# Shared PSUM banks in the mixer of a two-block model, and 30 convolution taps handed to the attention loop

## The chip, the cores and the metric

The kernel runs on one core of a Trainium2 chip. What counts is the device time of one execution in microseconds (us). Three executions of the kernel before took 4014.26, 4025.6 and 4031.81 us, the median is 4025.6 us. In the profile PE is TensorE's matmuls, PEld its weight loads, DVE is VectorE, ACT ScalarE, POOL GpSimd and SP the engine that issues most DMAs.

## The reference

Two blocks run one after the other on 512 tokens of width 1024. The change touches the second one only, in both of its layers. A layer there is a mixer followed by an MLP, and the mixer has three branches that read the same normalized input:

```python
h = rms_norm_2(x, pre_mix_w[l])
u = h @ w_in[l]
(u_conv, dq, dk, dv, gqkv, gz, b_f, b_b, a_f, a_b) = jnp.split(u, offs, axis=-1)
y_conv  = conv_module(u_conv, ...)      # 256 channels, gate, depthwise conv of 31 taps, layer norm, silu
y_diff  = diff_attention(dq, dk, dv, ...)  # 6 heads, two softmaxes each, o = (p0 - lam*p1) @ v
y_delta = gated_deltanet(gqkv, gz, ...)    # 6 heads, both directions, chunks of 64
y = jnp.concatenate([y_conv, y_diff, y_delta], axis=-1) @ w_out[l]
x = x + rms_norm_2(y, post_mix_w[l])
```

In the delta branch each chunk of 64 tokens needs a triangular solve (`u`, `w`), and a scan carries a state over the 8 chunks:

```python
v_new = u_i - w_i @ state
o     = qg_i @ state + aqk_i @ v_new
state = state * gl_i + kdec_i.T @ v_new
```

## The kernel before

**Stages of the mixer.** `second(l)` writes one mixer as a program in this order, where the numbers 0, 1, 2 are pairs of delta heads: the gates and the projections of pair 0; `delta_prep(0)`, its rest and the projections of pair 1; `delta_prep(1)` and its rest; `conv_proj`; `delta_uw(0)`; the projections of pair 2; `conv_taps`; `delta_prep(2)`; `delta_scan(0)`; `delta_uw(1)`; two `dense_tok` (z and v, 384 columns each); `diff_proj` (q and k of the attention); `delta_out(0)`, `delta_scan(1)`, rest of 2, `delta_uw(2)`, `delta_out(1)`, `delta_scan(2)`, `delta_out(2)`; last `diff`, the differential attention in 24 blocks (6 heads times 4 query blocks), with `conv_norm` inside it after the second pair of heads. After that the output projection reads all branches from DRAM (`cat`).

**What sets the order.** The program is written in that order, but a scheduler (the tile context is opened with `schedule_with_timeline_sim=True`) then gives each engine its own fixed list of instructions. It prefers what is earlier in the program, and takes later work where the earlier is not ready or its tile has no free slot. A tile pool has slots by tag; the tiles of one tag share them. Each engine runs its list strictly in order.

**PSUM.** There are 8 banks of 128x512 words. In the mixer before they are four pools of two: `mm` (projections, the attention's values `po`), `fx` (two of the four `dense_tok` outputs, transposes after the short convolution, the attention's scores and its transposes), `ax` (nearly all of the delta branch) and `sA` (the running state of the scan). So the delta branch and the attention never ask for the same bank.

**The delta branch** is a chain. In `delta_uw` each of two directions runs: 32 small matmuls (L1559), a DVE copy `AT`, 64 matmuls (L1569, L1570), the DVE update `TZ` (L1571), then twice 8 matmuls (L1583), a DVE `Q`, 8 matmuls (L1592), a DVE `Z` (L1593), and 16 matmuls (L1604) that ACT evacuates. `delta_scan` has 416 matmuls of 64x64 as the trace counts them and 7 steps that go PE, copy on DVE or ACT (L1650, L1652), PE. `delta_out` squares on ACT (L1694), makes a reciprocal root in some 13 short DVE instructions, multiplies, and transposes (L1707).

**The convolution** keeps two halves of 128 channels. Half z=0 is accumulated by one DVE instruction a tap (L1743, 30 of them after a first one on ACT), half z=1 by ACT (L1746, into the one buffer `cm`) and POOL (L1747).

**The attention.** A block is: two score matmuls into `fx` (L1840), per score one DVE instruction that adds the bias and takes the extreme (L1842) and one ACT exponential (L1844), the combination of the two softmaxes (on DVE L1862, in every third block ACT L1859 and POOL L1860), four transposes into `fx` (L1866), an ACT copy `dat`, and four matmuls with the values (L509). The loop runs one block ahead:

```python
scores(0)
for b in range(nb):
    if b + 1 < nb:
        scores(b + 1)
    outputs(b)
```

Of the kernel before, what the change touches and what calls it, by code (L numbers as in the profile page):

```python
# [9 lines left out]
F32 = mybir.dt.float32  # L10
# [3 lines left out]
AF = mybir.ActivationFunctionType  # L14
ALU = mybir.AluOpType
AX = mybir.AxisListType
PSUM = bass.MemoryType.PSUM
P = 128
# [103 lines left out]
class Rows:  # L122


    def __init__(self, a, b, c0=0, c1=768):
        self.t, self.c0, self.c1 = (a, b), c0, c1
# [32 lines left out]
class Slots:  # L159
# [6 lines left out]
    def tile(self, shape, dt, tag, name, bufs=1):  # L166
        n = int(np.prod(shape[1:]))
        if n < P:
            return self.pool.tile(shape, dt, tag=tag, name=name, bufs=bufs)
        t = self.slots[self.n % len(self.slots)][:, :n]  # L170
        self.n += 1
        names = "abcd"[:len(shape) - 1]
        return t.rearrange(f"p ({' '.join(names)}) -> p {' '.join(names)}", **dict(zip(names, shape[1:])))


class Kern:
# [12 lines left out]
    def tap(self, name, ap):  # L189
        if self._tap is not None and name in self._tap:  # L190
            self.nc.sync.dma_start(self._tap[name], ap)
# [1536 lines left out]
    def conv_taps(self, l, pool, hd):  # L1728
        nc = self.nc
        hp = pool.tile([P, 2, 544], F32, tag="hp", name="hp")  # L1730
        nc.gpsimd.memset(hp[:, :, 0:15], 0.0)
        nc.gpsimd.memset(hp[:, :, 527:544], 0.0)
        nc.sync.dma_start(hp[:, :, 15:527], hd)
        acc = pool.tile([P, 2, 512], F32, tag="cacc", name="cacc")
        for z in range(2):
            w = lambda t: self.dw[:, l, t, z:z + 1]
            a = acc[:, z]
            bias = self.vec("conv_dw_b_2", 2 * l + z, 1)
            nc.scalar.activation(a, hp[:, z, 0:512], AF.Identity, bias=bias, scale=w(0))
            for t in range(1, 31):  # L1740
                v = hp[:, z, t:t + 512]
                if z == 0:
                    nc.vector.scalar_tensor_tensor(out=a, in0=v, scalar=w(t), in1=a, op0=ALU.mult, op1=ALU.add)  # L1743
                else:
                    m = pool.tile([P, 512], F32, tag="cm", name="cm", bufs=1)
                    nc.scalar.activation(m, v, AF.Copy, scale=w(t))  # L1746
                    nc.gpsimd.tensor_tensor(out=a, in0=a, in1=m, op=ALU.add)  # L1747
        self.load["act"] += 31 * 480
        self.load["dve"] += 31 * 600
        self.load["pool"] += 31 * 1200  # L1750
        return acc

    def conv_norm(self, l, pool, acc, cat):
        nc = self.nc
# [37 lines left out]
                        nc.sync.dma_start(qk[f][z, g], x)  # L1792
                self.dense_fm(self.I["w_in_2"][l], [(c0 + P * f, P)], [hsrc], ev)

    def diff(self, l, pool, qk, vd, cat, between):

        nc = self.nc
# [27 lines left out]
        def scores(b):  # L1827
            hd, qb = b // 4, b % 4
            if qb == 0:
                head(hd)  # L1830
            s = heads[hd]
            if b % 2 == 0:
                blocks[b // 2] = (self.p_raw.tile([P, 2048], F32, tag="raw", name="dP").rearrange("p (q m c) -> p q m c", q=2, m=2),
                                  self.p_whl.tile([P, 1024], F32R, tag="wl", name="dat").bitcast(F32).rearrange("p (q k c) -> p q k c", q=2, k=4))
            pe = blocks[b // 2][0][:, b % 2]
            o0 = 384 - P * qb
            for m in range(2):
                ps = self.psf()
                t = s["qk"][m]
                nc.tensor.matmul(ps, t[:, qb * P:(qb + 1) * P], t[:, 512:], start=True, stop=True)  # L1840
                mx = s["mx"][:, qb, m:m + 1]
                nc.vector.tensor_tensor_reduce(out=pe[:, m], in0=ps, in1=s["bias"][:, o0:o0 + 512], scale=1.0, scalar=3.0e38,  # L1842
                                               op0=ALU.add, op1=ALU.min, accum_out=mx)
                nc.scalar.activation(pe[:, m], pe[:, m], AF.Exp, bias=mx, scale=-1.0, accum_out=s["sm"][:, qb, m:m + 1])  # L1844
            self.load["dve"] += 1300
            self.load["act"] += 1050
# [33 lines left out]

        nb = 24
        scores(0)
        for b in range(nb):
            if b + 1 < nb:
                scores(b + 1)
            outputs(b)

    def second_consts(self, pool, tmp):
        nc, I = self.nc, self.I
# [84 lines left out]
    def second(self, l):  # L1974
        tc, nc, I = self.tc, self.nc, self.I
        pd = self.p_dram
        w = I["w_in_2"][l]
# [4 lines left out]
        qk = [pd.tile([2, 4, P, 512], F32, tag=f"qk{l}{f}", name="qk") for f in range(3)]  # L1982
        cat = pd.tile([P, KT, 512], F32, tag=f"cat{l}", name="cat")
        p_ps = ExitStack()
        self.pd, self.pf, self.px, psa = (p_ps.enter_context(tc.tile_pool(name=f"{t}{l}", bufs=2, space=PSUM))
                                          for t in ("mm", "fx", "ax", "sA"))
        p_cv, cv, p_hs = self.p_cv, self.cv, self.p_hs
        nc.sync.dma_start(xs, self.x)
        self.p_x.close()
# [36 lines left out]
        self.conv_proj(l, pool, hs, hd)  # L2026
        uw(0)
        tok[2] = self.delta_proj(l, 2, pool, hs)
        acc = self.conv_taps(l, cv, hd)
        self.level(*BAL[1])  # L2030
        prep(2)
        scan(0)
# [13 lines left out]
        self.level(0, 0, 100)  # L2046
        out(2)
        self.level(*BAL[2])
        self.diff(l, rb, qk, vd, cat, lambda f: self.conv_norm(l, rb, acc, cat) if f == 1 else None)
        p_rb.close()  # L2050
        p_cv.close()
        p_dl.close()
# [309 lines left out]
```

## Time and profile before

| | |
|---|---|
| three runs, median | 4025.6 us (4014.26 to 4031.81) |
| profiled execution | 4036.42 us, its span 4034.6 us |
| PE, DVE, ACT, POOL busy | 3704.7, 2440.8, 1571.0, 1669.0 us |
| first mixer, gates to the last attention output | 2267 to 2673 us |
| second mixer, the same | 3167 to 3571 us |

The rows quoted further down are of one execution. A row "x30: 735/752/2862, 2331.5 to 2395.9" means 30 instructions, their shortest, median and longest duration in ns, and the start of the first and of the last in us from the span's start. PE's busy time is modelled from pipelined matmuls; a stretch with a granted clock (PEclk) of 1.00 runs at 2.4 GHz, one with 0.50 at 1.2 GHz.

### The profile page before, as it was taken

Reading aid. Unit: us, or ns where it says so; the run is one execution under the profiler, and the core shown is the slowest. Engines: PE = TensorE matmul, PEld = TensorE weight load, DVE = VectorE, ACT = ScalarE, POOL = GpSimd, SP = SyncE. Lnnn points to the kernel's source line nnn. Section 1 sums busy time; section 2 is a strip of 40 time slices with the busy share of each in tenths; the row PEclk is TensorE's granted clock in tenths of the full one; section 3 lists DMA queues with packets and bytes.
Section 4 is the critical chain, followed back from the end, with each engine's and each line's share of the span. In section 5 each row is a group of like instructions: output and inputs, shape, how many; then the busy total and the mean of one; then the engine's idle time right before and its main releaser. Section 6 shows DMA issues by size and latency. Waiting matters only on the chain. (4 is left out here: it accounts for less than half of the span.)

```text
span 4034.6 us, 67160 instructions
## 1 busy us (share of the span) xinstructions
PE 3704.7 (92%) x27441; PEld 3287.6 (81%) x27441; DVE 2440.8 (60%) x4507; ACT 1571.0 (39%) x2654; POOL 1669.0 (41%) x1168
## 2 busy tenths in 40 slices
PE   8999989989998999997999988878999988878998
PEld 6888767989998788887999876768988776778988
DVE  6454566665666333336776684548767685558665
ACT  4544255323223222223343543444434443344433
POOL 2221225455553223233666454215554363115654
PEclk8999879989999999998999987879999887878999
DMA  6322444112222212121232433132334333132333
GB/s 208 93 77 78 155 130 157 43 53 65 72 73 77 66 58 71 60 84 51 84 115 88 118 99 119 52 113 94 105 105 122 92 101 104 55 123 92 105 97 112
DMA packets 420364, 379.79 MB, mean 94 GB/s; under 512 B 64586, under 2 KB 366169, under 8 KB 419161
## 3 DMA queue, kind: packets, MB, share of 16 engines
q1 hardware_dynamic: 414490, 367.01, 29.4%
q10 hardware_dynamic: 5567, 8.49, 0.6%
q8 instruction: 216, 3.54, 0.4%
q14 instruction: 91, 0.75, 0.1%
HBM read 332.21 MB, written 43.25 MB: 93 GB/s over the span
## 5 line engine op out<-in xcount | busy, mean ns | idle before, releaser
L206 ACT CAST wh<-raw 128x1024 fp32r<-128x1024 f32 (+2 forms) x441 | 444.6, 1014 | 630.9 <-PE mm L486 277.6
L233 POOL TENSOR_TENSOR wl<-raw,wh 128x1024 fp32r<-128x1024 f32 (+2 forms) x196 | 468.1, 2397 | 530.7 <-ACT wh L206 476.5
L233 DVE TENSOR_TENSOR wl<-raw,wh 128x1024 fp32r<-128x1024 f32 (+1 forms) x268 | 378.1, 1415 | 189.1 <-ACT wh L206 176.4
L485 PE MATMUL mm<-Hh,wh 128*128 128x512 f32 (+1 forms) x1256 | 417.5, 335 | 15.3 <-DVE x L1033 12.9
L487 PE MATMUL mm<-Hh,wl 128*128 128x512 f32 (+1 forms) x1256 | 417.0, 333 | 0.5 <-DVE wl L233 0.5
L486 PE MATMUL mm<-Hl,wh 128*128 128x512 f32 (+1 forms) x1256 | 416.3, 332 | 0.0
L485 PEld LDWEIGHTS mm<-Hh,wh 128*128 128x128 f32 x1256 | 238.7, 190 | 42.9 <-DVE x L1033 14.3
L487 PEld LDWEIGHTS mm<-Hh,wl 128*128 128x128 f32 x1256 | 238.8, 190 | 26.1 <-DVE wl L233 0.7
L486 PEld LDWEIGHTS mm<-Hl,wh 128*128 128x128 f32 x1256 | 239.0, 190 | 24.3
L485 PE MATMUL mm<-hh,wh 128*128 128x512 f32 (+1 forms) x640 | 231.9, 366 | 16.4 <-DVE hh L208 6.9
L509 PE MATMUL mm<-hl,wh 128*128 128x256 f32 (+1 forms) x808 | 231.5, 290 | 6.4 <-DVE hl L1960 6.3
L509 PE MATMUL mm<-hh,wl 128*128 128x256 f32 (+1 forms) x808 | 231.6, 290 | 5.5 <-DVE wl L233 4.1
L487 PE MATMUL mm<-hh,wl 128*128 128x512 f32 (+1 forms) x640 | 227.2, 357 | 2.8 <-POOL wl L233 2.8
L486 PE MATMUL mm<-hl,wh 128*128 128x512 f32 (+1 forms) x640 | 229.0, 359 | 0.6 <-DVE hl L698 0.6
L509 PE MATMUL mm<-hh,wh 128*128 128x256 f32 (+1 forms) x808 | 218.4, 288 | 6.5 <-ACT hh L1968 3.2
L206 ACT CAST wh<-s 128x1024 fp32r<-128x1024 f32 (+1 forms) x128 | 106.9, 835 | 267.4 <-PE mm L486 137.6
L509 PE MATMUL mm<-th,wh 128*128 128x256 f32 (+1 forms) x644 | 195.3, 305 | 8.1 <-ACT wh L206 5.5
L509 PE MATMUL mm<-th,wl 128*128 128x256 f32 (+1 forms) x644 | 197.3, 307 | 3.1 <-DVE wl L233 3.1
L1033 DVE SCALAR_TENSOR_TENSOR x<-mm,mod,x 128x512 f32<-128x512 f32 (+1 forms) x224 | 138.2, 630 | 99.9 <-PE mm L487 99.4
L509 PE MATMUL mm<-tl,wh 128*128 128x256 f32 (+1 forms) x644 | 195.3, 303 | 0.6 <-DVE tl L233 0.6
L233 POOL TENSOR_TENSOR Hl<-o,Hh 128x1024 fp32r<-128x1024 f32 (+3 forms) x76 | 140.9, 1856 | 92.6 <-ACT Hh L206 91.1
L509 PEld LDWEIGHTS mm<-hl,wh 128*128 128x128 f32 (+1 forms) x808 | 155.8, 193 | 9.7 <-DVE hl L1960 7.7
(737 smaller groups left out, 10886.8 us busy)
## 6 DMA issues: line engine op xcount, KB each, us to landing
raw<-in_w_ff_dram SPq DMA_DIRECT2D x68, 1024.0 KB
raw<-in_ffn_w_in_dram SPq DMA_DIRECT2D x88, 512.0 KB
raw<-in_mod_w_dram SPq DMA_DIRECT2D x40, 1024.0 KB
raw<-in_odd_w_in_dram SPq DMA_DIRECT2D x24, 1024.0 KB
raw<-in_ffn_w_out_dram SPq DMA_DIRECT2D x19, 1024.0 KB
raw<-in_w_in_dram SPq DMA_DIRECT2D x38, 512.0 KB
dqk<-qk SPq DMA_DIRECT2D x48, 256.0 KB
raw<-in_w_out_dram SPq DMA_DIRECT2D x12, 768.0 KB
```

The lines of the kernel that those rows point to most:

```text
L206: nc.scalar.copy(hi, src)
L233: i = (nc.vector if e == "dve" else nc.gpsimd).tensor_tensor(out=out, in0=a, in1=b, op=op)
L485: mm(ps, ah, bh, start=first, stop=False)
L486: mm(ps, ah, bl, start=False, stop=False)
L487: mm(ps, al, bh, start=False, stop=last)
L509: i = self.nc.tensor.matmul(out, lhsT, rhs, start=start, stop=stop, skip_group_check=True)
L1033: self.nc.vector.scalar_tensor_tensor(out=x[:, ct, :n], in0=ps, scalar=gate[:, ct:ct + 1], in1=x[:, ct, :n], op0=ALU.mult, op1=ALU.add)
```

## The change

The pools `fx`, `ax` and `sA` become one pool with the single tag `any` and six banks; `mm` keeps its two. Whatever tag a caller names, its tile comes from those six. The scores run two blocks ahead in place of one. `conv_taps` starts both halves on ACT, issues the whole half z=1 as before, and returns the 30 DVE taps of z=0 as functions; `diff` calls two of them after each of its first 15 blocks. Names and arithmetic stay; in the changed file lines are 10 later up to `conv_taps`, the tap on DVE is L1756, the score matmul L1846, the transposes of the attention L1872.

```diff
+class OneTag:
+    def __init__(self, pool):
+        self.pool = pool
+
+    def tile(self, shape, dt, tag, name):
+        return self.pool.tile(shape, dt, tag="any", name=name)
...
+        w = lambda t, z: self.dw[:, l, t, z:z + 1]
         for z in range(2):
-            w = lambda t: self.dw[:, l, t, z:z + 1]
-            a = acc[:, z]
-            bias = self.vec("conv_dw_b_2", 2 * l + z, 1)
-            nc.scalar.activation(a, hp[:, z, 0:512], AF.Identity, bias=bias, scale=w(0))
-            for t in range(1, 31):
-                v = hp[:, z, t:t + 512]
-                if z == 0:
-                    nc.vector.scalar_tensor_tensor(out=a, in0=v, scalar=w(t), in1=a, op0=ALU.mult, op1=ALU.add)
-                else:
-                    m = pool.tile([P, 512], F32, tag="cm", name="cm", bufs=1)
-                    nc.scalar.activation(m, v, AF.Copy, scale=w(t))
-                    nc.gpsimd.tensor_tensor(out=a, in0=a, in1=m, op=ALU.add)
...
+            nc.scalar.activation(acc[:, z], hp[:, z, 0:512], AF.Identity, bias=self.vec("conv_dw_b_2", 2 * l + z, 1), scale=w(0, z))
+        for t in range(1, 31):
+            m = pool.tile([P, 512], F32, tag="cm", name="cm", bufs=1)
+            nc.scalar.activation(m, hp[:, 1, t:t + 512], AF.Copy, scale=w(t, 1))
+            nc.gpsimd.tensor_tensor(out=acc[:, 1], in0=acc[:, 1], in1=m, op=ALU.add)
...
+        def tap(t):
+            nc.vector.scalar_tensor_tensor(out=acc[:, 0], in0=hp[:, 0, t:t + 512], scalar=w(t, 0), in1=acc[:, 0], op0=ALU.mult, op1=ALU.add)
+        return acc, [lambda t=t: tap(t) for t in range(1, 31)]
...
         scores(0)
+        scores(1)
         for b in range(nb):
-            if b + 1 < nb:
-                scores(b + 1)
+            if b + 2 < nb:
+                scores(b + 2)
             outputs(b)
+            for f in fill[2 * b:2 * b + 2]:
+                f()
...
-        self.pd, self.pf, self.px, psa = (p_ps.enter_context(tc.tile_pool(name=f"{t}{l}", bufs=2, space=PSUM))
-                                          for t in ("mm", "fx", "ax", "sA"))
+        self.pd, ps = (p_ps.enter_context(tc.tile_pool(name=f"{t}{l}", bufs=n, space=PSUM)) for t, n in (("mm", 2), ("any", 6)))
+        self.pf = self.px = psa = OneTag(ps)
```

The instruction lists of the engines show where the scheduler puts all this. The first place is PE at the end of the first mixer's delta branch. Before, scores (L1840, `fx<-dqk`), attention transposes (L1866) and values (`mm<-dv,dat`) stand among the last pair's `delta_prep` (L1446, L1463, L1475) and the first scan (`sA`, L1637):

```order
L509 MATMUL sA<-U,kd 64x64 x14
L1840 MATMUL fx<-dqk 128x512 x2
L1446 MATMUL ax<-gd,dm 128x512
L1463 MATMUL ax<-eb,dm 128x512
L1475 MATMUL ax<-kT 64x64 x8
L1866 MATMUL fx<-ident,dP 128x128 x4
L1840 MATMUL fx<-dqk 128x512
L509 MATMUL mm<-dv,dat 128x64 x4
L1840 MATMUL fx<-dqk 128x512
L1866 MATMUL fx<-ident,dP 128x128 x4
L1475 MATMUL ax<-kT 64x64 x8
L1637 MATMUL ax<-kd,W 64x64 x16
```

Now the first score of the mixer stands behind the last matmul of the last scan (`ax<-kd,qg`) and behind the transposes of the last `delta_out` (L1717):

```order
L519 MATMUL ax<-U,Aq 64x64 x15
L519 MATMUL ax<-kd,qg 64x64 x28
L1717 MATMUL ax<-ident,OI 128x128 x4
L1846 MATMUL fx<-dqk 128x512 x6
L1872 MATMUL fx<-ident,dP 128x128 x4
L1846 MATMUL fx<-dqk 128x512 x2
L1872 MATMUL fx<-ident,dP 128x128 x4
```

All 48 scores, 96 transposes and 96 value matmuls of the mixer have moved behind the whole delta branch; from there on PE's list holds only the attention and the convolution's norm.

The second place is PE at the end of `delta_uw(0)` and the start of the first scan. Before, projections (L485 to L487) stand around them:

```order
L485 MATMUL mm<-hh,wh 128x512
L486 MATMUL mm<-hl,wh 128x512
L1559 MATMUL ax<-TZ,A_20716 32x32 x32
L509 MATMUL sA<-U,kd 64x64 x14
L487 MATMUL mm<-hh,wl 128x512
L485 MATMUL mm<-hh,wh 128x512
L486 MATMUL mm<-hl,wh 128x512
```

Now that stretch, from the last half of `delta_uw(0)` through `delta_prep(2)` (L1441 to L1485) and the scan, has none:

```order
L1614 MATMUL ax<-VB,Z 64x128 x14
L1441 MATMUL ax<-ident,tokk 128x128 x4
L1456 MATMUL ax<-gd,dm 128x512 x2
L1473 MATMUL ax<-eb,dm 128x512
L1485 MATMUL ax<-kT 64x64 x16
L519 MATMUL sA<-U,kd 64x64 x14
L1647 MATMUL ax<-kd,W 64x64 x16
L519 MATMUL sA<-U,kd 64x64 x14
```

and the next projection, one of `dense_tok` into `fx`, comes only when `delta_uw(1)` has taken its last tile:

```order
L1593 MATMUL ax<-TZ,KK 32x32 x8
L1602 MATMUL ax<-Z,Q 32x32 x8
L1614 MATMUL ax<-VB,Z 64x128 x2
L495 MATMUL fx<-wh,hh 128x384
L496 MATMUL fx<-wl,hh 128x384
```

Behind that row PE's list has 144 matmuls of 384 columns and 144 of 512 (`diff_proj`) in one run, with no delta work in it but the rest of L1614.

The third place is DVE around the taps. Before, they stand among the first solve (`chT`, `chX`) and the short convolution (`pc`):

```order
L1393 SCALAR_TENSOR_TENSOR pc<-mm,cw,pc 128x511
L1743 SCALAR_TENSOR_TENSOR cacc<-hp,dw,cacc 128x512
L1520 TENSOR_TENSOR chX<-chX,chT 128x10x6
L645 SCALAR_TENSOR_TENSOR dy<-dnt,dy 128x16
L1394 SCALAR_TENSOR_TENSOR pc<-mm,cw,pc 128x511
L1743 SCALAR_TENSOR_TENSOR cacc<-hp,dw,cacc 128x512
```

Now they stand among the second solve and the `Q` and `Z` of the first half of `delta_uw(0)`:

```order
L1756 SCALAR_TENSOR_TENSOR cacc<-hp,dw,cacc 128x512
L1530 TENSOR_TENSOR chX<-chX,chT 128x12x4
L1603 TENSOR_SCALAR Z<-ax 32x8x32
L1595 TENSOR_TENSOR Q<-ax,beta 32x256
L1756 SCALAR_TENSOR_TENSOR cacc<-hp,dw,cacc 128x512
L1528 TENSOR_TENSOR chT<-chG,chX 128x55
L1603 TENSOR_SCALAR Z<-ax 32x8x32
```

All 30 come before the second half of `delta_uw(0)`, none beside an attention block. Between the gates' first DVE instruction and the last tap DVE's list has 207 instructions before and 213 now.

## Rows read from the trace of the kernel before

**Rows 1.** The page, busy time of each engine.
```profile
PE 3704.7 (92%) x27441; PEld 3287.6 (81%) x27441; DVE 2440.8 (60%) x4507; ACT 1571.0 (39%) x2654; POOL 1669.0 (41%) x1168
```

**Rows 2.** Windows by stage: stretch, length, busy by engine, PEclk, DMA share, GB/s.
```profile
2267.00:2331.00 64.00, 60.74 (x330) 47.77 (x329) 47.13 (x110) 38.27 (x57) 28.79 (x18) 0.97 0.45 118
2331.00:2396.00 65.00, 52.11 (x385) 45.90 (x384) 63.36 (x97) 34.72 (x51) 40.77 (x28) 0.84 0.33 82
2396.00:2463.00 67.00, 60.92 (x732) 48.99 (x720) 28.30 (x54) 23.72 (x40) 34.92 (x26) 0.95 0.48 151
2463.00:2673.00 210.00, 173.95 (x2818) 147.68 (x2818) 128.16 (x382) 85.20 (x196) 45.28 (x40) 0.73 0.23 72
...
3361.00:3571.00 210.00, 174.25 (x2818) 147.64 (x2818) 126.69 (x382) 85.08 (x196) 43.12 (x37) 0.71 0.23 71
```

**Rows 3.** Single lines in the first mixer: count, durations, first and last start.
```profile
L1743 DVE SCALAR_TENSOR_TENSOR cacc<-hp,dw,cacc x30: 735/752/2862, 2331.5 to 2395.9; 128x512 f32<-128x512 f32 x30
L1604 PE MATMUL ax<-VB,Z x192: 269/320/473, 2421.3 to 2610.9; 64*64 64x128 f32 x192
L1786 DVE SCALAR_TENSOR_TENSOR dlo<-mm,dhi x6: 691/692/692, 2422.0 to 2462.3; 128x512 fp32r<-128x512 f32 x6
L1842 DVE CUSTOM_DVE_ANT_0 dP<-fx,abias x48: 664/688/692, 2463.5 to 2665.3; 128x512 f32<-128x512 f32 x48
L1874 DVE TENSOR_TENSOR do<-mm,drs x6: 418/425/425, 2520.4 to 2672.9; 128x256 f32<-128x256 f32 x6
```

**Rows 4.** The transposes and products of `delta_prep(2)` on PE.
```profile
L1431 PE MATMUL ax<-ident,tokk x4: 272/272/328, 2459.5 to 2459.9; 128*128 128x128 f32 x4
L1475 PE MATMUL ax<-kT x32: 311/311/366, 2471.4 to 2479.7; 64*64 64x64 f32 x32
```

**Rows 5.** Windows of the three scans (2479, 2556, 2613) and of the attention's end.
```profile
2479.00:2503.00 24.00, 19.52 (x382) 18.59 (x382) 11.38 (x45) 4.76 (x13) 2.54 (x2) 0.63 0.21 41
2556.00:2571.00 15.00, 13.77 (x398) 13.56 (x398) 7.99 (x28) 5.50 (x16) 3.58 (x3) 0.93 0.06 21
2613.00:2629.00 16.00, 14.34 (x392) 13.83 (x391) 7.06 (x29) 5.03 (x14) 2.31 (x2) 0.89 0.13 45
...
2640.00:2673.00 33.00, 27.04 (x108) 22.39 (x106) 18.41 (x54) 16.35 (x31) 3.12 (x4) 0.50 0.44 148
```

**Rows 6.** Timeline of the second half of `delta_uw(2)`: start, length, instruction.
```profile
2597.64 0.75 PE L1559 MATMUL ax<-TZ,A 32*32 32x32 f32 x64
...
2602.22 0.69 DVE L1571 TENSOR_TENSOR TZ<-TZ,ax 128x512 f32<-128x512 f32 x1 [1.55 <-PE ax L1570]
...
2609.17 1.96 PE L1604 MATMUL ax<-VB,Z 64*64 64x128 f32 x30
```

**Rows 7.** Timeline of projection matmuls that follow each other at clock 1.00.
```profile
2322.10 0.39 PE L485 MATMUL mm<-hh,wh 128*128 128x512 f32 x1
2322.33 0.40 PE L486 MATMUL mm<-hl,wh 128*128 128x512 f32 x1
2322.56 0.39 PE L487 MATMUL mm<-hh,wl 128*128 128x512 f32 x1
```

**Rows 8.** Timeline of `delta_out(2)`, its square on ACT and its transposes on PE.
```profile
2629.65 0.63 ACT L1694 ACTIVATE hsq<-OI 128x512 f32<-128x512 f32 x1
...
2639.77 0.86 PE L1707 MATMUL ax<-ident,OI 128*128 128x128 f32 x4 [0.23 <-DVE OI L233]
```

**Rows 9.** DVE's groups in 2460 to 2680: busy us, mean ns, idle before.
```profile
L1842 DVE CUSTOM_DVE_ANT_0 dP<-fx,abias 128x512 f32<-128x512 f32 x48 | 32.5, 686 | 11.2 <-PE fx L1840 10.1 <-POOL abias L1809 0.6
L1862 DVE SCALAR_TENSOR_TENSOR dP<-dP,drs 128x512 f32<-128x512 f32 x16 | 14.2, 885 | 0.4
...
L1856 DVE SCALAR_TENSOR_TENSOR drs<-dsm,nlam,drs 128x1 f32<-128x1 f32 x24 | 6.0, 250 | 0.5
...
L1842 DVE DVE_READ_ACCUMULATOR2_ANT dmx<- 128x1 f32 x48 | 4.0, 82 | 0.0
L1854 DVE RECIPROCAL drs<-dsm 128x2 f32<-128x2 f32 x24 | 3.9, 162 | 9.9 <-ACT dP L1844 9.9
```

**Rows 10.** PE's groups in 2642 to 2673, the attention without the delta branch.
```profile
L509 PE MATMUL mm<-dv,dat 128*128 128x64 f32 x64 | 14.9, 421 | 2.7 <-ACT dat L243 2.7
L1866 PE MATMUL fx<-ident,dP 128*128 128x128 f32 x24 | 6.6, 430 | 2.9 <-POOL dP L1860 2.6 <-DVE dmx L1842 0.4
L1840 PE MATMUL fx<-dqk 128*128 128x512 f32 x8 | 5.9, 759 | 0.2 <-ACT dat L243 0.2
```

More of the change, by code (lines that the diff above doesn't have):

```diff
@@ L1734, in conv_taps @@
         acc = pool.tile([P, 2, 512], F32, tag="cacc", name="cacc")
+        w = lambda t, z: self.dw[:, l, t, z:z + 1]
         for z in range(2):
-            w = lambda t: self.dw[:, l, t, z:z + 1]
-            a = acc[:, z]
-            bias = self.vec("conv_dw_b_2", 2 * l + z, 1)
-            nc.scalar.activation(a, hp[:, z, 0:512], AF.Identity, bias=bias, scale=w(0))
-            for t in range(1, 31):
-                v = hp[:, z, t:t + 512]
-                if z == 0:
-                    nc.vector.scalar_tensor_tensor(out=a, in0=v, scalar=w(t), in1=a, op0=ALU.mult, op1=ALU.add)
-                else:
-                    m = pool.tile([P, 512], F32, tag="cm", name="cm", bufs=1)
-                    nc.scalar.activation(m, v, AF.Copy, scale=w(t))
-                    nc.gpsimd.tensor_tensor(out=a, in0=a, in1=m, op=ALU.add)
-        self.load["act"] += 31 * 480
-        self.load["dve"] += 31 * 600
+            nc.scalar.activation(acc[:, z], hp[:, z, 0:512], AF.Identity, bias=self.vec("conv_dw_b_2", 2 * l + z, 1), scale=w(0, z))
[3 more added lines that the diff above has]
+            nc.gpsimd.tensor_tensor(out=acc[:, 1], in0=acc[:, 1], in1=m, op=ALU.add)
+        self.load["act"] += 32 * 480
         self.load["pool"] += 31 * 1200
-        return acc
+        def tap(t):
+            nc.vector.scalar_tensor_tensor(out=acc[:, 0], in0=hp[:, 0, t:t + 512], scalar=w(t, 0), in1=acc[:, 0], op0=ALU.mult, op1=ALU.add)
+        return acc, [lambda t=t: tap(t) for t in range(1, 31)]
     def conv_norm(self, l, pool, acc, cat):
@@ L1793, in diff_proj, with diff @@
                 self.dense_fm(self.I["w_in_2"][l], [(c0 + P * f, P)], [hsrc], ev)
-    def diff(self, l, pool, qk, vd, cat, between):
+    def diff(self, l, pool, qk, vd, cat, between, fill):
         nc = self.nc
@@ L2028, in second @@
         tok[2] = self.delta_proj(l, 2, pool, hs)
-        acc = self.conv_taps(l, cv, hd)
+        acc, taps = self.conv_taps(l, cv, hd)
         self.level(*BAL[1])
@@ L2048, in second @@
         self.level(*BAL[2])
-        self.diff(l, rb, qk, vd, cat, lambda f: self.conv_norm(l, rb, acc, cat) if f == 1 else None)
+        self.diff(l, rb, qk, vd, cat, lambda f: self.conv_norm(l, rb, acc, cat) if f == 1 else None, taps)
         p_rb.close()
```

## The prediction

> **What bounds the kernel now.** I read the engine totals first, then windows by stage, then single lines, timelines and groups. PE is busy 92% of the span [rows 1], but its matmuls are pipelined, so the stages decide. Only the two mixers change. The first runs from 2267 to 2673 us, the second, with the same figures within 2 us, from 3167 to 3571.
>
> Its windows show three different limits [rows 2]. From 2267 to 2331 PE is busy 60.74 of 64 us at clock 0.97: projections. From 2331 to 2396 DVE is busy 63.36 of 65 us, and the 30 taps of L1743 start exactly there, 2331.5 to 2395.9, 752 ns each [rows 3]: DVE sets the pace. The long stretch from 2463 to 2673 has PE 173.95 and DVE 128.16 busy of 210 us at a mean clock of 0.73: the delta chain and the attention run interleaved, and each fills gaps of the other. At its end, from 2640 to 2673, the attention is alone: 33 us for six blocks (24 transposes, four a block [rows 10]), PE 27.04 busy, clock 0.50 [rows 5], that is the 1.2 GHz level.
>
> **What the change does here.** The words say that taps go beside attention blocks. The order says otherwise: all 30 stay ahead of the second half of `delta_uw(0)`, and DVE has 213 instructions up to the last of them against 207. What moves is the attention. With one tag its scores must wait for all delta tiles that the program names earlier. So per mixer PE's list falls into five parts that follow each other. I add them up in the first mixer's time, then double.
>
> *A, to the end of `delta_uw(0)`.* The last tap starts at 2395.9 [rows 3] because DVE is saturated. Six more of some 210 instructions, of the same kinds, leave it at 2396. Behind it come the second half's last `TZ` (0.69), `Q`, `Z` and L1604 (1.96 [rows 6]), with their hand-overs about 8 us: 2404. Bounds: 2398, if the second half has run up to its last `Z` beside the taps; 2412, if it starts only then, which is little more than the measured half, 2597.64 to 2611.13, 13.5 us with attention in between [rows 6].
>
> *B, `prep(2)`, `scan(0)`, `delta_uw(1)` without projections.* `prep(2)` took 20.2 us from the transposes of `tokk` at 2459.5 to the last L1475 at 2479.7 [rows 4], with scores and values between. Without them I take 14, bounds 8 and 20. The scans took 24, 15 and 16 us at clocks 0.63, 0.93 and 0.89 [rows 5]. One scan alone leaves PE waiting at each of its seven steps, so I expect it nearer to the slow one: 20, bounds 15 and 24. `delta_uw(1)` is two halves of 13.5 us or less, partly overlapped: 20, bounds 17 to 24. Sum 54: 2458.
>
> *C, the projections in one run.* 144 matmuls of 512 columns at 0.23 us each, from start to start at clock 1.00 [rows 7], are 34 us; 144 of 384 columns, by the ratio 0.175 each, 25. With 3 us for a first stretch at the lower clock: 62, bounds 58 and 66: 2520. Before, the last of this work was taken from PSUM at 2462.3 (L1786 [rows 3]). The weight loads for it stand on SP behind `prep(2)`'s small loads, which are issued some 30 us earlier; I cost that at nothing, and at up to 5 us if SP is late, inside the sum's range.
>
> *D, the rest of the delta branch alone.* `delta_out(0)`: the last one needs 10.1 us from its square (2629.65) to its transposes (2639.77) [rows 8], and it is in front of `scan(1)` on PE: 10. `scan(1)` 18 (15 to 24), 2 to `delta_uw(2)`, that itself 20, and `scan(2)` with `delta_out(2)` 27 (2613 to 2640 before). Sum 77, bounds 68 and 91: 2597. Before, this point was 2640, so the delta branch ends 43 us earlier.
>
> *E, the attention alone.* In its place all 24 blocks are still to come; before, 18 of them had been done beside the delta branch. Three prices can be read. At the measured rate of 33 us for six blocks [rows 5], 5.4 a block, it is 130. By PE's busy time at 1.2 GHz, without gaps, a block is 4.45 us: values 14.9 us for 64 records, eight a block as the trace counts them, 1.86; transposes 6.6 us for six blocks, 1.1; scores 5.9 us for four blocks, 1.48 [rows 10]. That is 107 for 24 blocks, and about half of it at the higher level. By DVE it lies between 74 (18.41 us busy for six blocks [rows 5], times four) and 102 (the 128.16 of the interleaved stretch [rows 2] less the 26.43 of its three scans [rows 5], which still holds `delta_uw` and `delta_out`); 32.5 and 4.0 for the scores, 14.2 for the combinations, 6.0 and 3.9 for the small ones are 61 of it [rows 9], the norms, `conv_norm` and splits of the output weights the rest. I take the middle, 88. For E I take 100, between DVE's 88 and PE's 107. With scores two blocks ahead and six banks, most of PE's waits should go: `fx` to DVE (10.1 us of idle on DVE [rows 9]) and PE on `dP` and `dat` (2.6 and 2.7 [rows 10]). DVE is then late next, at 88, and a denser PE should see the higher clock part of the time. End: 2697, where the last `do` now starts at 2672.9 [rows 3].
>
> So +24 a mixer, +48 for both. The Trainium skill ("Perfetto Trace Analysis", section Optimization Strategy) says that where the most-contended engine changes between regimes, interleaving the regimes may improve performance. The trace agrees: the interleaved 210 us have clock 0.73, the attention alone 0.50; by that rule the change, which takes the interleaving out, loses.
>
> **Small edits.** Both halves of the taps now start on ACT at once: one instruction earlier by one place, nothing, hidden behind DVE. The load figures in `conv_taps` are overwritten by the next `level`, so they move nothing. A few table loads fewer on ACT, which is busy 85 of 210 us [rows 2]: nothing on the path, at most a few us. Output stores and loads of `qk` keep their order; with 77 us of D between, they are hidden.
>
> The profiled execution took 4036.4 us (span 4034.6 and 1.8 around it): 4084. The median of the runs is 4025.6, 10.8 lower, so the forecast is 4074.
>
> **Rivals.**
> R1, faster: the banks really free things. For it: PE's and DVE's waits on `fx` above. The Trainium skill, same page and section, says that consistent bubbles can mean too little PSUM for the next tile; rows 9 show such a wait, but only 10.1 us of it in 210. All lower ends: A 2398, B 44, C 58, D 68, E 88: 2656, so −17 a mixer, −34: about 3992. Against it: the scan's steps are dependences, not slots.
> R2, much slower: the attention alone holds its measured rate, 130, because ACT's and DVE's hand-overs and not slots set it and PE stays at 1.2 GHz: 2727, +54 a mixer: 4134. For it: it is the only rate that the trace shows. Against it: in these 33 us only one block was ahead, and `conv_norm`, which comes once a mixer, was among the six blocks.
> R3, no change: B and D come in 15 us shorter together and E at 90: 2672, the same to within 10 us a mixer.
> R4, the taps do run beside the blocks: 30 by 0.752 us are 22.6 of DVE in E, and the same less in A. The order rules it out.
>
> The point that decides is where the first score (L1840 now, L1846 then) starts and how long E is: faster than before needs a start before 2573 with E at 100, or E under 76 (DVE's lower bound) with a start at 2597.
>
> **How the numbers follow.** A run of this kernel can tell about 0.5%, 20 us, from no change. Forecast (4035 to 4108: +10 to +82) 0.50, R1 0.20, R2 0.13, R3 0.17. R4 gets nothing. Faster: R1's 0.20. Same: R3 and the forecast's lower edge of 0.06, 0.23. Slower: the rest, 0.57. The range leaves out half of R1 and the upper half of R2, and holds the forecast: 3998 to 4134.
>
> **What would show it.** A: last tap near 2396, last L1614 (now L1604) of `delta_uw(0)` at 2398 to 2412. B and C: a run of projections from about 2458 to 2520 at clock near 1.00, and none in the scan before. D: scans of 18 us or more, first score near 2597. E: 100 us, DVE at 85% or more, clock between 0.5 and 1.0. If the first score comes before 2575, the delta branch needed less time alone than I think; if E is 80 or below, the attention was bound by its banks and the forecast is wrong in sign.

## The result and the profile after

The changed kernel takes 4180.99 us (median of four runs, 4170.38 to 4186.56) against 4025.34 for the kernel before: ratio 1.0387, 95% interval 1.0353 to 1.042. It is slower, as forecast, but by 155.7 us and not by 48; the time lies 47 us above the upper end of the range. The profiled execution has a span of 4174.0 us, 139.4 over the one before: the profiled execution before took 11 us more than the median of its kernel, this one 5 less.

Engine totals of the profile after, in answer to [rows 1]:

```profile
PE 3701.5 (89%) x27441; PEld 3304.1 (79%) x27441; DVE 2443.1 (59%) x4507; ACT 1560.6 (37%) x2647; POOL 1664.6 (40%) x1168
```

No engine but PEld, which overlaps PE, is busy more than 3 us longer than before; PE is busy 3701.5 us against 3704.7. So the 139 us are nearly all waiting. They lie in the two mixers: from the copy of the gates (the DVE copy `gf`, the mark from which places are counted below) to the last `do` the first takes 484.0 us (406.6 before) and the second 473.9 (404.6), together 147 more; the rest of the kernel is some 7 us shorter. The first mixer by the parts A to E of the prediction, windows of the profile after (length, then busy us of PE, PEld, DVE, ACT, POOL, then PEclk, DMA share, GB/s):

```profile
2331.00:2397.00 66.00, 43.44 (x662) 35.39 (x661) 62.52 (x103) 24.27 (x38) 34.76 (x25) 0.82 0.25 57
2397.00:2426.00 29.00, 15.90 (x145) 11.94 (x147) 19.60 (x42) 12.60 (x24) 15.93 (x13) 0.64 0.18 37
2426.00:2455.00 29.00, 18.73 (x388) 17.51 (x381) 16.30 (x48) 8.96 (x19) 13.29 (x11) 0.66 0.17 33
2455.00:2481.00 26.00, 19.94 (x595) 17.97 (x594) 9.25 (x16) 1.88 (x5) 8.10 (x7) 0.63 0.06 8
2481.00:2545.00 64.00, 63.81 (x320) 55.99 (x318) 10.82 (x13) 17.59 (x26) 10.61 (x5) 0.96 0.49 154
2545.00:2565.00 20.00, 2.36 (x28) 2.03 (x29) 4.72 (x17) 1.70 (x3) 4.19 (x4) 0.57 0.66 222
2565.00:2581.00 16.00, 14.73 (x428) 14.31 (x426) 5.66 (x15) 4.68 (x12) 0.00 (x0) 0.90 0.08 26
2581.00:2615.00 34.00, 26.22 (x708) 23.72 (x703) 12.23 (x32) 3.17 (x9) 4.39 (x4) 0.65 0.06 18
2615.00:2632.00 17.00, 10.25 (x312) 10.04 (x309) 7.13 (x24) 4.21 (x11) 0.00 (x0) 0.83 0.01 2
2632.00:2745.00 113.00, 80.93 (x395) 73.09 (x393) 72.50 (x226) 62.21 (x141) 19.66 (x18) 0.64 0.28 98
```

Read it against [rows 2, 5]: the row of 64 us is the projections, with PE full at clock 0.96. In the first row DVE is full with the taps. In the rows of the delta chain and of the attention no engine is full but PE in the 16 us of `scan(1)` (14.73 busy, clock 0.90); in the others that PE works through the clock is 0.63 to 0.66, and 0.83 for `scan(2)`. The 20 us from 2545 are nearly empty on all engines.

Single lines of the first mixer (instruction, count, shortest/median/longest ns, first to last start), in answer to [rows 3]:

```profile
L1756 DVE SCALAR_TENSOR_TENSOR cacc<-hp,dw,cacc x30: 737/752/2321, 2342.1 to 2396.6; 128x512 f32<-128x512 f32 x30
L1792 DVE SCALAR_TENSOR_TENSOR dlo<-mm,dhi x6: 684/691/694, 2518.1 to 2555.6; 128x512 fp32r<-128x512 f32 x6
L1846 PE MATMUL fx<-dqk x48: 387/628/776, 2632.2 to 2712.2; 128*128 128x512 f32 x48
L1880 DVE TENSOR_TENSOR do<-mm,drs x6: 411/424/425, 2653.3 to 2745.1; 128x256 f32<-128x256 f32 x6
```

The last tap is 136 us behind the gates' copy (130 before), the last `dlo` 294 (196 before), the first score 371 (189 before), behind the whole delta branch. That branch itself ends at the same place: its last transposes start 371 us after the gates, 374 before. These 3 us are the difference of two large shifts. Before, all projections stood ahead of the end of `delta_uw(0)`; now 288 of their matmuls, 61 us of PE, come behind it. So `delta_uw(0)` ends 151 us behind the gates and not 193. From there to the last transposes the branch takes 220 us and not 181, with these projections and the empty stretch behind them in it as rows of their own, 64 and 20 us. The other 136 us, without the attention, are fewer than the 181 beside it.

### The profile page after: what moved, and what is told of

Same layout as the page of the kernel before. It is cut to its first block, busy times and chain, and to the rows that moved or that the text cites. A ratio compares the mean times of both kernels' runs of the same rounds, so it can differ in the third digit from the quotient of the medians.

```text
span 4174.0 us, 67214 instructions
## 1 busy us (share of the span) xinstructions
PE 3701.5 (89%) x27441; PEld 3304.1 (79%) x27441; DVE 2443.1 (59%) x4507; ACT 1560.6 (37%) x2647; POOL 1664.6 (40%) x1168
## 5 line engine op out<-in xcount | busy, mean ns | idle before, releaser
L495 PEld LDWEIGHTS mm<-Hh,wh 128*128 128x128 f32 x1256 | 238.9, 190 | 43.3 <-DVE x L1043 14.5
L495 PEld LDWEIGHTS mm<-hh,wh 128*128 128x128 f32 x640 | 124.5, 195 | 53.7 <-DVE pc L1404 8.4
```

The source lines that it names most:

```text
L495: mm(ps, ah, bh, start=first, stop=False)
```

## The experiments

Below, "mixer" is the stretch from the gates' copy on. Ratios are to the kernel before on the same chip. Where two numbers are given for a place they are of the first and second mixer, in us behind the gates' copy.

### The pools alone, and all but the pools

The first experiment puts the four pools back into the changed kernel, the second puts the one tag into the kernel before.

```diff
 # first, in the changed kernel; the second is the same edit the other way, with the class OneTag, in the kernel before
-        self.pd, ps = (p_ps.enter_context(tc.tile_pool(name=f"{t}{l}", bufs=n, space=PSUM)) for t, n in (("mm", 2), ("any", 6)))
-        self.pf = self.px = psa = OneTag(ps)
+        self.pd, self.pf, self.px, psa = (p_ps.enter_context(tc.tile_pool(name=f"{t}{l}", bufs=2, space=PSUM))
+                                          for t in ("mm", "fx", "ax", "sA"))
```

> The changed kernel with the four old PSUM pools of two banks; scores two blocks ahead and the 30 taps as functions inside the attention's loop stay. Theory S (the one shared tag hands its slots out in program order, and that alone takes the projections and the attention out of the delta branch): the loss goes, 4025 us within 25; the last stretch in which the attention is alone is again some 30 to 50 us, not 113. Theory L (the look-ahead of two and the place of the taps cost the time): it stays near 4180.

> The kernel before with only the pools changed: six banks under one tag; scores one block ahead, convolution as before. Theory S: the whole loss is here, 4180 us within 25 (130 to 180 over before), and the attention's first score comes behind the last delta_out in the mixer, near 2630. Theory L: 4025 within 25.

Measured: with four pools 4020.36 us, ratio 0.9978 (0.9962 to 0.9994). The one tag alone: 4193.32 us, ratio 1.0418 (1.0402 to 1.0435). The scores in the first mixer, with four pools and then with the one tag alone:

```profile
L1846 PE MATMUL fx<-dqk x48: 387/498/1414, 2438.9 to 2633.6; 128*128 128x512 f32 x48
```

```profile
L1850 PE MATMUL fx<-dqk x48: 390/628/776, 2641.1 to 2725.7; 128*128 128x512 f32 x48
```

The 48 scores take 195 us beside the delta branch or 85 alone, and the 195 cost less. The whole loss is the tag's, theory L falls. What is left of the change gains 0.2%. The second run tells one thing more: with one block ahead the attention alone, from the first score to the last `do`, takes 110 and 113 us, and with two ahead, in the changed kernel, 113 and 106. So the second block ahead was worth some 2 us there.

### fx out of the shared tag

```diff
-        self.pd, ps = (p_ps.enter_context(tc.tile_pool(name=f"{t}{l}", bufs=n, space=PSUM)) for t, n in (("mm", 2), ("any", 6)))
-        self.pf = self.px = psa = OneTag(ps)
+        self.pd, self.pf, ps = (p_ps.enter_context(tc.tile_pool(name=f"{t}{l}", bufs=n, space=PSUM)) for t, n in (("mm", 2), ("fx", 2), ("any", 4)))
+        self.px = psa = OneTag(ps)
```

> The changed kernel with fx as a pool of its own with two banks again and four banks shared by ax and sA alone. Theory S in its narrow form (what matters is that the attention and dense_tok do not ask for the delta branch's slots): 4025 us within 30, since the attention runs beside the delta branch again. Theory S in its wide form (any shared tag ties a stage to the one written before it, here scan state to delta tiles too): some 4060 to 4100. Theory L: near 4180.

Measured: 4027.38 us, ratio 1.0005 (0.9989 to 1.0021). So it is not sharing as such: a tag shared by `ax` and `sA`, which belong to one branch, costs at most the 7 us between this run and the four pools. What costs is that `fx` is under the tag: the attention and two of the `dense_tok` outputs then ask for the slots of a branch that the program names earlier. That the slots go by the program's order is read from the instruction lists. The place of the work moved here too: the first score comes 222 us behind the gates (189 before), the delta branch's last transposes 342 (374 before), the last `do` 409 (407). The delta branch ends 32 us earlier and the mixer does not.

### Two taps really beside each block

```diff
-        def tap(t):
-            nc.vector.scalar_tensor_tensor(out=acc[:, 0], in0=hp[:, 0, t:t + 512], scalar=w(t, 0), in1=acc[:, 0], op0=ALU.mult, op1=ALU.add)
+        def taps(b, sm):
+            wc = pool.tile([P, 2], F32, tag="wc", name="wc", bufs=2)
+            nc.vector.scalar_tensor_tensor(out=wc, in0=sm, scalar=0.0, in1=self.dw[:, l, 1 + 2 * b:3 + 2 * b, 0], op0=ALU.mult, op1=ALU.add)
+            for k in range(2):
+                t = 1 + 2 * b + k
+                nc.vector.scalar_tensor_tensor(out=acc[:, 0], in0=hp[:, 0, t:t + 512], scalar=wc[:, k:k + 1], in1=acc[:, 0], op0=ALU.mult, op1=ALU.add)
...
-            for f in fill[2 * b:2 * b + 2]:
-                f()
+            if b < 15:
+                fill(b, heads[b // 4]["sm"][:, b % 4])
... # and the four old pools
```

> The changed kernel with the four old pools, and the two taps of a block held to their block: their weights come from a 128x2 DVE instruction that also reads (times zero) the block's row sums; 15 such instructions of about 0.25 us are added a mixer. This is what the change's words say, and what its instruction order does not do. Theory D (from 2331 to 2396 DVE sets the pace, and the attention's stretch has DVE free for 82 of 210 us): the stretch before gets shorter by most of 22.6 us, the attention's takes them at little cost: 10 to 20 us less a mixer, 3985 to 4010 us. Rival: PE is late next in that stretch (52 of 65 us busy), so at most 5 us a mixer are won and the attention's chain gives them back: 4025 within 15.

Measured: 4054.06 us, ratio 1.008 (1.0062 to 1.0097), 34 us above the same kernel with the taps in their early place. It lies outside both theories; the rival, that nothing is won, was the nearer. The taps in the first mixer, then the window from the first score to the last `do`:

```profile
L1760 DVE SCALAR_TENSOR_TENSOR cacc<-hp,wc,cacc x30: 727/744/1758, 2465.5 to 2601.8; 128x512 f32<-128x512 f32 x30
```

```profile
2444.00:2682.00 238.00, 183.45 (x2851) 157.01 (x2849) 152.45 (x429) 87.23 (x199) 43.98 (x38) 0.70 0.23 73
```

The same window of the first experiment:

```profile
2439.00:2654.00 215.00, 176.62 (x2902) 151.28 (x2901) 131.05 (x385) 89.30 (x203) 45.98 (x41) 0.75 0.26 81
```

In the stretch that they left, the last `dlo` comes 189 us behind the gates against 194 and 197 in the first experiment: 5 to 7 us won of 22. In the stretch that they went to, first score to last `do` takes 238 us against 215 in the first mixer and 235 against 216 in the second: 19 to 23 us more. The taps, 30 of 0.744 us, are 22.3, and the 15 added weight instructions, of 142 ns in the median, some 2. DVE was busy there for only 131 of 215 us, and still most of it was paid. Its list is in order, so a tap can delay the engine that waits for what stands behind it: in the first mixer PE's wait for DVE's `gd` is 11.1 us (2.1 in the first experiment) and for `dmx`, ahead of scores and transposes, 12.6 (6.1).

### The empty 20 us at 2545

In the changed kernel the timeline around the hole is (start, length, instruction, in brackets the wait before it):

```profile
2544.43 0.39 PE L497 MATMUL mm<-hh,wl 128*128 128x512 f32 x1
...
2547.20 0.62 ACT L1704 ACTIVATE hsq<-OI 128x512 f32<-128x512 f32 x1
...
2555.62 0.69 DVE L1792 SCALAR_TENSOR_TENSOR dlo<-mm,dhi 128x512 fp32r<-128x512 f32 x1 [9.35 <-DMA qk<-dhi]
2556.22 0.68 DVE L1705 TENSOR_REDUCE hss<-hsq 128x8 f32<-128x512 f32 x1
...
2562.64 1.12 PE L1717 MATMUL ax<-ident,OI 128*128 128x128 f32 x4 [17.82 <-POOL OI L243]
```

PE's last projection ends at 2544.8. The projections `q` and `k` are converted on ACT (`dhi`) and DVE (`dlo`) and stored to DRAM (`qk`), from three buffers. The square `hsq` of `delta_out(0)` had to wait on ACT behind the last `dhi`; its sum `hss` then waited on DVE behind a `dlo` that waited 9.35 us for a buffer being stored. PE stood at the transposes, with `scan(1)` behind them. Two experiments took the two parts of this.

```diff
-        out(0)
         scan(1)
+        out(0)
```

> The changed kernel with two calls swapped in the program: scan(1) before out(0). In the changed kernel PE stands 17.8 us before delta_out(0)'s transposes in each mixer, with scan(1) queued behind them. Theory W (that wait is only PE's place in the order): scan(1) fills it, 13 to 18 us less a mixer, 4145 to 4155 us. Rival Q (the square of delta_out(0) is late because ACT's and DVE's lists stand at the q and k conversions, which wait for their buffers' stores; the scan's copies run on the same two engines and stand there too): at most 5 us less a mixer, 4170 to 4181.

Measured: 4162.0 us, ratio 1.0337 (1.0309 to 1.0364), 19 us below the changed kernel and between the two theories. The two intervals overlap, the single executions do not (4157 to 4168 and 4170 to 4187), and in the profiles the mixers end 11 and 6 us earlier. The scan does run ahead, and then meets the same DVE list: its `GI` stands behind the last `dlo`. The profile names no releaser for DVE's 9.25 us before that `dlo`; in the changed kernel it is the store. DVE there, and PE's longest wait in that place:

```profile
2568.78 0.69 DVE L1792 SCALAR_TENSOR_TENSOR dlo<-mm,dhi 128x512 fp32r<-128x512 f32 x1 [9.25 <-issue]
2569.39 0.68 DVE L1648 TENSOR_TENSOR GI<-ax,GI 128x512 f32<-128x512 f32 x1
```

```profile
PE sA L519 <- DVE GI L1648: 9.0, 1, 9.0
```

```diff
-... tag="pc", name="dhi", bufs=3)    # and the four other tiles of the tag
+... tag="pc", name="dhi", bufs=5)
```

> The changed kernel with five buffers in place of three under the tag pc, from which the q and k conversions are stored. Theory Q (at the end of the projections ACT and DVE wait for stores to free these buffers, the last conversion comes 11 us after PE's last projection, and delta_out(0)'s square and sums stand behind it): that wait goes, PE's 17.8 us before the transposes fall to about 8, 8 to 11 us less a mixer, 4155 to 4165 us. Rival M (the DMA engines are the limit at 0.66 of their time, more buffers only move the wait): at most 3 us less a mixer, 4175 to 4185.

Measured: 4194.22 us, ratio 1.0427 (1.0399 to 1.0456), above both theories and 13 us over the changed kernel, whose interval it overlaps. The store wait did go. What ended DVE's idle time before `dlo` in the five-buffer kernel (us, times) is no longer the DMA, which ended 24.9 us of it in the changed kernel:

```profile
L1792 DVE SCALAR_TENSOR_TENSOR dlo<-mm,dhi x6: 687/692/692, 2535.3 to 2562.6; 128x512 fp32r<-128x512 f32 x6
its engine sat idle before it (us, times) until:
  ACT dhi L1791: 22.4, 5
```

The six conversions follow each other in 27 us instead of 37. But PE still waits 15.9 us for the transposes:

```profile
2570.46 1.96 POOL L1815 TENSOR_SCALAR abias<-dist 128x896 f32<-128x896 f32 x2 [33.19 <-DMA dist<-in_k_dist_dram]
2572.50 1.04 POOL L243 TENSOR_TENSOR OI<-OI,hy 128x512 f32<-128x512 f32 x1
...
2576.56 1.26 POOL L243 TENSOR_TENSOR OI<-OI,zt 128x512 f32<-128x512 f32 x1 [3.01 <-DMA zt<-zd]
2577.87 1.11 PE L1717 MATMUL ax<-ident,OI 128*128 128x128 f32 x4 [15.94 <-POOL OI L243]
```

This does not mean that the stores held only 2 us. Two other transfers took their place, on POOL. The last `hy` is done at 2567.7, and its product starts at 2572.50, behind `abias`, which waits for the load `dist` that ACT issues only behind the last `dhi`; then POOL waits for `zt`. Without these two, some 7 us by these lines, PE's wait would be near 9 (an estimate), as theory Q had it. And the buffers changed the order elsewhere (48 `dense_tok` matmuls now stand ahead of `delta_uw(0)`, whose first product comes 148 us behind the gates and not 121), so the time as a whole says nothing of the stores alone.

### The attention alone

```diff
-            if b % 3 == 0:
+            if b < 0:
                 nc.scalar.activation(pe[:, 1], pe[:, 1], AF.Copy, scale=rs[:, 1:2])
```

> The changed kernel with the combination of the two softmaxes always on DVE; before, every third block went over ACT and POOL. In the attention's 113 us PE waits 16.4 us for POOL's result, and DVE is busy 72.5. Theory P (the hand-over ACT, POOL, PE holds up the blocks, PE in order behind it): 8 instructions of 0.9 us more on DVE and some 16 us of waits less, 5 to 10 us less a mixer, 4160 to 4172 us. Rival V (DVE's own list sets the pace): 7 us more a mixer, 4190 to 4200.

Measured: 4182.1 us, ratio 1.0391 (1.0361 to 1.042), no difference from the changed kernel, so neither theory holds. PE's longest wait in the attention, in the changed kernel and then in this one:

```profile
PE fx L1872 <- POOL dP L1866: 16.4, 5, 6.1
```

```profile
PE fx L1872 <- DVE dP L1868: 12.9, 7, 3.5
```

The transposes wait for the combined softmax whoever combines it. The wait has another name and is little shorter; first score to last `do` takes 111 and 108 us against 113 and 106.

### Other shares of the banks, buffers, and the look-ahead

```diff
 # e7 (fx three), in the changed kernel:  ("mm", 2), ("fx", 3), ("any", 3) for ax and sA
 # e8, the same line:  ("mm", 2), ("fx", 3), ("ax", 2), ("sA", 1)
 # e12, the same line: ("mm", 2), ("fx", 2), ("ax", 3), ("sA", 1)
 # e10: four pools of two, and bufs=5 under pc;  e11: the kernel before with scores two ahead
```

> The changed kernel with fx as a pool of three banks and three banks shared by ax and sA. By its order the attention's scores end inside the last delta_uw. Theory H (the more of the attention stands beside the delta branch, the shorter the mixer): 5 to 15 us less a mixer than with fx of two, 3995 to 4015 us. Rival K (the delta branch is the long chain, and PE and DVE in order put attention work in front of it; three banks for ax and sA hold it up as well): 4035 to 4070.

> The changed kernel with four pools again, fx with three banks and sA with one. By its order the attention is done before the second half of the last delta_uw. Theory H: 3995 to 4015 us. Rival K: the delta branch ends later for each block put in front of it, and a scan with one bank for its two directions waits at each step: 4050 to 4100.

> The changed kernel with four pools: fx two banks, ax three, sA one. Measured so far with fx of two and sA of two: the delta branch's last solve products start 352 us after the gates, the attention's last value step 401. With fx of three and sA of one: 364 to 387 and 383 to 386, at the same time in all. Theory B (the later of the two branches ends the mixer, so a third bank for the delta branch with fx at two does not help unless the attention gets nearer): 4015 within 6, the attention's end still near 400. Rival T (with the third bank the delta branch leaves PE and DVE sooner and the attention follows): 3995 to 4008.

> The four old pools, scores two ahead, taps as functions (as in the first experiment), with five buffers under pc. Theory Q carried over (in the interleaved form too the stores pace the last projections, and the first score waits for them): the attention starts 5 to 10 us earlier and the mixer ends 3 to 8 us earlier, 4005 to 4014 us. Rival I (in the interleaved form other work stands beside that wait): 4020 within 6, as with three buffers.

> The kernel before with one thing changed: scores two blocks ahead. Theory A (the small gain with the four old pools, ratio 0.9978, is the look-ahead's): ratio 0.996 to 0.999, 4012 to 4022 us. Rival F (it comes from the convolution's order): ratio 0.999 to 1.002.

Measured, with the last transposes of the delta branch and of the attention in each mixer:

| kernel | us | ratio (interval) | delta | attention |
|---|---|---|---|---|
| before | 4025.3 | 1 | 374, 371 | 417, 415 |
| four pools, first experiment | 4020.4 | 0.9978 (0.9962 to 0.9994) | 377, 380 | 409, 413 |
| e7, fx 3, shared 3 | 4049.8 | 1.0053 (1.003 to 1.0075) | 423, 415 | 416, 395 |
| e8, fx 3, ax 2, sA 1 | 4021.6 | 0.999 (0.9975 to 1.0005) | 398, 412 | 394, 398 |
| e12, fx 2, ax 3, sA 1 | 4046.2 | 1.0039 (1.0026 to 1.0053) | 392, 391 | 424, 424 |
| e10, four pools, five buffers | 4015.2 | 0.9975 (0.9959 to 0.9991) | 376, 375 | 406, 406 |
| e11, only two ahead | 4016.5 | 0.9978 (0.9963 to 0.9994) | 378, 378 | 411, 412 |
| changed kernel | 4181.0 | 1.0387 (1.0353 to 1.042) | 371, 368 | 492, 482 |

Compare by the ratios: the runs are from several chips. The later of the two branches ends the mixer. With a third bank for `fx` the attention gets ahead and the delta branch becomes the later one: theory H falls in e7, and e8 lies between H and K. Each of these also takes a bank from the delta branch, so what the third bank gave and what the missing one cost are not told apart. The same holds for e12, where `sA` has one bank: both branches end later than in the first experiment, against theory B, which had the attention near 400, and rival T; why is left open. Two ahead alone gives what the first experiment gave, which is theory A: within the intervals the gain of the rest of the change is the look-ahead's. Five buffers do not gain beyond that by these intervals, though the attention ends 3 to 7 us earlier than with three. The best versions are a quarter of a per cent below the kernel before.

## Why the prediction was wrong

**What held.** The order was read rightly: the taps do not move beside the attention, the one tag takes projections and attention out of the delta branch, and PE's list becomes five parts one behind the other. The experiments with the pools alone and with `fx` apart show the one tag, with `fx` under it, to be the cause of the whole loss. R1 and R3 did not come: no other share of the banks gained more than a quarter of a per cent. R4 was rightly given nothing: the last tap starts at 2396.6, ahead of all scores.

**What failed** is the size: terms of the sum were too small, in the parts A, B, D and E. The largest is `delta_uw` alone, put at 20 us and measured at 31.9 and 31.4. The gates' copy came 5.2 us earlier in the execution after; with that added, in the first mixer:

| part | forecast | measured | miss |
|---|---|---|---|
| A, end of `delta_uw(0)` | 2404 | 2417 | 13 |
| B, `prep(2)`, `scan(0)`, `delta_uw(1)` | 54 | 70 | 16 |
| C, projections | 62 | 63 | 1 |
| D, to the first score | 77 | 87 | 10 |
| E, the attention alone | 100 | 113 | 13 |

That is 53 us too little in this mixer; with the 24 forecast it makes the 77 measured. In the second mixer 69 were measured.

*B and D: `delta_uw` alone.* The step that failed is "two halves of 13.5 us or less, partly overlapped: 20". From its first matmul to its last product `delta_uw(1)` took 31.9 us and `delta_uw(2)` 31.4. The 13.5 was the second half of `delta_uw(2)` in the trace before, 2597.64 to 2611.13. The first half, just ahead of it, took 19.9 there, and the two did not overlap. The first half's timeline, and both halves as windows (fields as above):

```profile
2576.05 0.83 PE L1559 MATMUL ax<-TZ,A 32*32 32x32 f32 x64 [0.33 <-DVE o2n L644]
...
2592.38 3.57 PE L1604 MATMUL ax<-VB,Z 64*64 64x128 f32 x30
```

```profile
2576.05:2595.95 19.90, 18.43 (x331) 15.21 (x331) 14.49 (x38) 9.11 (x22) 5.25 (x4) 0.74 0.15 56
2597.64:2611.12 13.48, 12.75 (x347) 10.62 (x346) 9.20 (x26) 6.32 (x15) 4.31 (x4) 1.00 0.21 58
```

I had priced both halves by the quicker one. The whole of `delta_uw(2)`, window before and window after:

```profile
2576.05:2611.12 35.07, 32.88 (x689) 27.28 (x689) 24.01 (x64) 16.08 (x39) 9.55 (x8) 0.85 0.17 54
```

```profile
2581.28:2612.71 31.43, 23.65 (x620) 21.22 (x618) 11.00 (x28) 2.53 (x7) 4.39 (x4) 0.62 0.06 19
```

So it did get shorter without the attention, as I expected, but by 3.6 us and not by 15; `delta_uw(1)` went from 46.6 us (from 2503.02 in the trace before) to 31.9 (from 2457.00 in the one after). The timeline of the first half in D, and the start of the second:

```profile
2585.32 0.33 PE L1579 MATMUL ax<-AT,TZ 32*32 32x32 f32 x7 [3.28 <-DVE AT L1572]
...
2588.13 1.06 PE L1593 MATMUL ax<-TZ,KK 32*32 32x32 f32 x16 [0.86 <-DVE TZ L1581]
...
2594.04 0.63 PE L1569 MATMUL ax<-TZ,A 32*32 32x32 f32 x26
2594.59 3.67 PE L1614 MATMUL ax<-VB,Z 64*64 64x128 f32 x28
```

The halves take 17.0 and 18.7 us and overlap by 4. The chain of PE, DVE, PE leaves PE idle for 7.8 of 31.4 us, and the granted clock is 0.62, where the half that I took as the measure had 1.00: 28 products of L1614 take 3.67 us here against 1.96 for 30 in [rows 6]. The half of 19.9 us shows that this is not a matter of standing alone: beside the attention, its 30 products took 3.57. How much of the miss is clock and how much idle time was not separated.

`scan(0)` took 29 us at clock 0.66, over my upper bound of 24, but it was not alone on the other engines. PE waits for its copies `kd`, and these stand on DVE behind steps of the next triangular solve, which wait for a transfer:

```profile
2438.99 1.22 DVE L1528 TENSOR_TENSOR chT<-chG,chX 128x15 f32<-128x15 f32 x1 [5.00 <-DMA chG<-gdd]
...
2442.36 0.29 DVE L1660 COPY kd<-sA 64x128 f32<-64x128 f32 x1
...
2442.70 0.37 PE L519 MATMUL sA<-kd,GI 64*64 64x64 f32 x1 [2.85 <-DVE kd L1660]
```

`scan(1)`, right behind the transposes, took 16 at 0.90, 2 less than forecast.

*D: `delta_out(0)` at 10.* It took 20, since its chain went on only behind the last conversion of the projections. I had written that the stores of `qk` were hidden with 77 us of D between. That looked at who reads them, and not at who stands behind the conversions on ACT and DVE. The last `dlo` waited 9.35 us for a store, with `hss` right behind it; `hsq` was done at 2547.8 and `hss` started at 2556.2, so some 8 us of the hole are the stores' and the rest is mostly `delta_out`'s own length. After the swap of the two calls the scan stood at the same `dlo` for 9.0. D's miss is only 10, since `scan(2)` with `delta_out(2)` took 17 and not 27.

*A: the second half of `delta_uw(0)`.* The case was the forecast's own: the half runs beside the taps up to its last `TZ`, which DVE makes behind the last tap, and PE waits 9.5 us for it. But the last tap came 6 us later than forecast (2396.6, with the 5.2 added 2402), and from its start to the last product it took 15.5 us and not 8; twelve transposes of the short convolution stood ahead of the last products:

```profile
2396.62 0.74 DVE L1756 SCALAR_TENSOR_TENSOR cacc<-hp,dw,cacc 128x512 f32<-128x512 f32 x1
...
2398.71 0.67 DVE L1581 TENSOR_TENSOR TZ<-TZ,ax 128x512 f32<-128x512 f32 x1
2399.44 1.06 PE L1593 MATMUL ax<-TZ,KK 32*32 32x32 f32 x16 [9.50 <-DVE TZ L1581]
...
2406.25 2.82 PE L1410 MATMUL fx<-ident,pc 128*128 128x128 f32 x12
...
2409.00 3.07 PE L1614 MATMUL ax<-VB,Z 64*64 64x128 f32 x28
```

*E: the attention.* I expected two banks and one more block ahead to leave DVE full at 85%. It is busy 72.5 of 113 us (64%), PE 80.9 at clock 0.64. The largest groups, DVE and PE of the changed kernel (busy us, mean ns, idle before), in answer to [rows 9, 10]:

```profile
L1848 DVE CUSTOM_DVE_ANT_0 dP<-fx,abias 128x512 f32<-128x512 f32 x48 | 31.5, 684 | 14.5 <-PE fx L1846 14.5
```

```profile
L519 PE MATMUL mm<-dv,dat 128*128 128x64 f32 x192 | 36.5, 375 | 0.0
L1846 PE MATMUL fx<-dqk 128*128 128x512 f32 x48 | 23.7, 588 | 2.6 <-DMA dqk<-qk 2.6
L1872 PE MATMUL fx<-ident,dP 128*128 128x128 f32 x96 | 21.2, 368 | 22.9 <-POOL dP L1866 16.4 <-DVE drs L1862 4.0 <-DVE dP L1868 2.5
```

DVE's wait for `fx`, 10.1 us before, is 14.5 now: more banks did not remove it. In PE's list the scores stand behind transposes that wait (22.9 us idle before them), which would explain it; no run tested that. Nor did the second block ahead help much: one ahead, with the one tag alone, took 110 and 113 us for this stretch. So the rate of 130, read from the last six blocks, was too high for the whole attention even with one block ahead, and the waits that I took off for the second block stayed. The price 107, from PE's busy time at the lower level, was nearer than DVE's 88 and than my 100.

**The range** ended at R2's 4134, which moves E alone. All five parts missed on the same side: A and B passed their upper bounds, C and D stayed within theirs, and E passed the 107. The upper ends together, 2412, 68, 66, 91 and 107, give 2744, 71 over before and 142 for both mixers: 4168, still 13 below the result. The lower and upper sums also have slips: B's lower terms make 40 and not 44, and the terms written out for D make 71 to 87 and not 68 to 91. R2's 4134 with the misses of A, B and D, 39 a mixer, would be 4212, 31 over; its E of 130 was 17 a mixer too long.

## What to carry to other kernels

Before tiles of two branches are put under one tag, see which branch the program names first: here the slots went in that order, and the later branch lost all its overlap although six banks were shared. When a change takes work out from beside a dependent chain, price the chain by its whole measured length and not by its quickest part: `delta_uw(2)` took 35.1 us beside the attention and 31.4 alone, and its quicker half, 13.5 us, foretold 20. An engine that is busy 60% of a stretch may still have no room: see whether what waits for its results is on the chain. When a wait is removed and the time does not fall, look for the next wait in the same place before calling the first one cheap.

## What the runs showed of the hardware that was not expected

Taking PE's other work away from beside a dependent chain gave back less than that work's time. `delta_uw(2)` lost the 16 us of PE's attention work that stood inside it and became 3.6 us shorter. Beside the attention PE was busy 32.88 of 35.07 us at a granted clock of 0.85; alone it was busy 23.65 of 31.43 us at 0.62, between the levels of 1.2 and 2.4 GHz. The second mixer shows the same: 34.8 us at 0.81 before and 31.4 us at 0.57 after. It is not so in every stretch without the attention: `scan(1)` had 0.90 over 16 us, right behind 20 us in which PE was busy for 2.36. No run held the clock and took the attention away, so what the clock costs by itself is left open.
